# A hybrid decoder block on one core: the first feed-forward block by seven products, its second resident tile later, the residual's bias by DMA, the output sums behind an evacuation

## The chip, the core and the metric

The kernel runs on one core of a Trainium2 chip. The metric is the device time of one execution in microseconds (us); the time of a kernel is the median of its runs. The engines are named as in the profile: PE (TensorE matmul) and PEld (its weight loads), DVE (VectorE), ACT (ScalarE), POOL (GpSimd) and SP (SyncE); POOL and SP issue nearly all the DMAs here.

## The reference, cut to what matters

```python
proj = x @ w_in                      # x: 256 x 2048; w_in: 2048 x 9216
q, k, v, u, vb, ga, gb = split(proj)
attn = dilated_window_attention(q, k, v)           # 8 heads of 128
gmlp = gelu(u) * spatial(layer_norm(gelu(vb)))
merged = sigmoid(ga) * (attn @ w_proj_a) + sigmoid(gb) * (gmlp @ w_proj_b)
h = layer_norm(ALPHA * x + merged @ w_out)         # gain ln1_g, bias ln1_b
a = square(relu(h @ w_ff1 + b_ff1))                # 2048 -> 8192
y = layer_norm(ALPHA * h + a @ w_ff2 + b_ff2)      # 8192 -> 2048
```

All in float32 at a sequence of 256; 99% of the work is in the products with the weights, which are each read once.

## The kernel before, in words

**Products and splits.** A float32 product is made of three products of shorter floats: weight and activation are each split into a high part and a low part, and high x high, high x low and low x high are added up in PSUM. The weights come in chunks of 512 rows x 512 columns (`raw`, 1 MB, three buffers; SP loads chunk j+3 once chunk j is split, line 162). Half a chunk is a piece. A piece's split is two instructions into a ring buffer (`w`): ACT copies the high part (L188), DVE subtracts for the low part (L157, 128x1024). There are six ring buffers (`RING`), and some groups may use further tags while these lie free (`spare`, `wide`).

**Steps.** The program is a list of steps, each of one piece. Before each step the host loop (line 977) emits in this order: the splits that find a free buffer (`emit_splits`); the waiting high and low parts of activations (`rounds`: `hilo`, L93 on ACT and L94 on DVE); one waiting second half of an evacuation (`later`); then the step's matmuls (`run_step`) with the evacuation behind its group's last step; then what `at(step, ...)` has put down for the step. Every engine works its own stream in that order. So a split stands in the streams about six steps ahead of its use, and an evacuation behind what was emitted before it.

**PSUM.** Six banks named `mm`. A group with the weights stationary (`ws`) uses four, so the next group has two free banks and needs the first one's evacuation for its third: ACT copies half of the bank (L273, L275), DVE adds the other half (`sum`, L277).

**Order by stages.** Input projection, attention, gMLP; then for i in 0 to 3 the groups `w_pa` i and `w_pb` i, whose sigmoid gates make `merged`; the output projection; LayerNorm 1; and the feed-forward part in eight blocks of 1024 hidden units: two `ff1` groups a block (eight steps each, F below) and, one block later, `ff2` (E below).

**Seven products.** Of a 1024-row block of `ff2` (and of half of the output projection) the first two column chunks are eight products of 512 rows by 128 tokens by 512 columns. Where the block is in `SUMMED`, they are made by seven: P1 to P7, each on a sum of weights or of activations or both. The weight sums come from accumulating DMAs on POOL's queue into two resident tiles `b` 0 and `b` 1 (`held`): tile 0 is loaded (L624) and gets a further block added (L633) after each of P1, P5 and P6; tile 1 is loaded and gets one block added at once (`held_load`, L626), and serves P7. The activation sums (`ca`) are made by `sum_of_acts`: four DVE operations on 128x128 (`cb`, L576 to L579) for each of four tiles, and their high and low parts. `ORDER` says how P1 to P7 lie among F and E in a block; each P is two steps of six matmuls.

**What the change touches.** `SUMMED` is `range(1, NB - 1)`: block 0 is made by the plain eight products. Its `ff1` groups 2 and 3 come first, then 16 E steps. Between them stands the second residual: `residual2` on DVE makes `ALPHA * ln1_b + b_ff2` (part 0, L562) and then, for each token tile and column chunk, `y * ALPHA * ln1_g` (L565) and the addition of the former (L566); 4 + 8 + 8 operations of 128x512. Its three vectors are broadcast over the partitions by SP (`load_wide`, L556, 1 MB each), behind chunks of `ff1` group 2. The sums for the output projection are made in `ev_yb` when group 1's second half is worked (line 491).

Of the kernel before, what the change touches and what calls it, by code (L numbers as in the profile page):

```python
# [16 lines left out]
ALU = mybir.AluOpType  # L17
# [4 lines left out]
NT = S // P  # L22
# [4 lines left out]
G = 8  # L27
DB = G * 128
FF = 4 * D
CW = 512  # L30
# [5 lines left out]
NCT = CW // P  # L36
ORDER = ("F F F P1 F P1 F F F P5 F P5 F F F P6 F P6 F P3 P3 F P7 F P7 F "
         "E P2 E P2 E E P4 E P4 E E E").split()
WARM = (256, 256, 256, 128)
EARLY = 3  # L40
NBUCKET = 32
MAXDIST = 2048
ALPHA = 2.0 ** 0.25
# [28 lines left out]
def block_kernel(ctx: ExitStack, tc: tile.TileContext, xT, x, w_in, rel_bias, lnv_g, lnv_b, wsT, b_sp,  # L72
# [61 lines left out]
    def add_group(g, sizes=None):  # L134
        hs = add_pieces(g, sizes)
        for h in hs:
            add_step(h, "all", h == hs[0], h == hs[-1])
# [343 lines left out]
    def ev_yb(g):  # L481
        def fin(ot, s):
            if g == 0 and ot == 0:
                tiles["merged"] = quads("merged", [f"S1{i}" for i in range(4)])
            gt, d = tiles["G", g], tiles["merged"][g][:, ot, :]
            nc.vector.tensor_tensor(s, s, gt[:, 1, ot, :], op=ALU.mult)
            q = kept(ot) if g == 0 else s
            nc.vector.tensor_tensor(q, s, gt[:, 0, ot, :], op=ALU.add)
            rounds.append((hilo, d[:, :S], d[:, S:], q))
            if g == 1:  # L490
                sum_of_acts(("S6", "W"), ot, q)

        def ev(ot, p):
            later.append((fin, ot, halves(p)))
        return ev
# [58 lines left out]
    def load_wide(key, src, tag):  # L554
        tiles[key] = big.tile([P, D], F32, name="wide", tag=tag)
        nc.sync.dma_start(tiles[key], bcast(src, D))  # L556

    def residual2(c, part):
        sl = slice(c * CW, (c + 1) * CW)
        bb = tiles["b_ff2"][:, sl]  # L560
        if part == 0:
            nc.vector.scalar_tensor_tensor(bb, tiles["ln1_b"][:, sl], ALPHA, bb, op0=ALU.mult, op1=ALU.add)  # L562
        else:
            y = tiles["y", part - 1][:, sl]
            nc.vector.scalar_tensor_tensor(y, y, ALPHA, tiles["ln1_g"][:, sl], op0=ALU.mult, op1=ALU.mult)  # L565
            nc.vector.tensor_tensor(y, y, bb, op=ALU.add)  # L566

    def sum_of_acts(tags, ot, q):


        if ot == 0:
            for i in range(2):
                tiles["ca", i] = big.tile([P, 2, NCT, 2, P], F32R, name="ca", tag=tags[i])
        q0, t0, t1 = tiles["q", ot], slice(0, P), slice(P, S)
        cb = work.tile([P, 4, P], F32, name="cb", tag="pt")
        nc.vector.tensor_tensor(cb[:, 0], q0[:, t1], q[:, t1], op=ALU.subtract)  # L576
        nc.vector.tensor_tensor(cb[:, 2], q0[:, t0], q0[:, t1], op=ALU.subtract)
        nc.vector.tensor_tensor(cb[:, 1], cb[:, 0], q0[:, t0], op=ALU.subtract)
        nc.vector.tensor_tensor(cb[:, 3], q[:, t0], cb[:, 1], op=ALU.add)  # L579
        for i in range(2):  # L580
            d = tiles["ca", i][:, :, ot]
            rounds.append((hilo, d[:, :, 0], d[:, :, 1], cb[:, 2 * i:2 * i + 2]))

    def kept(ot):
        q = tiles["q", ot] = work.tile([P, S], F32, name="q0", tag="es"[ot // 2])
        return q
# [19 lines left out]
        return ev  # L606

    NB = FF // 1024
    SUMMED = range(1, NB - 1)

    def ff_unit(blk):
        return SimpleNamespace(w=w_ff2, row=blk * 1024, act=lambda r, k: tiles["a", 2 * blk + r][:, k, :],
                               tags=("S10", "S11"), acc="S12", key="ff", scale=None)

    def out_unit():
        return SimpleNamespace(w=w_out, row=0, act=lambda r, k: tiles["merged"][r][:, k, :],
                               tags=("S5", "A0"), acc="A1", key="out", scale=ALPHA)

    def held_load(u, i):

# [74 lines left out]
    def mixed(b):  # L697

        made = {"F": [ff1_group(2 * b), ff1_group(2 * b + 1)], "E": [ff2(b - 1, c) for c in (2, 3)]}
        prods = products(ff_unit(b - 1), ff_unit(b) if b in SUMMED else None)  # L700
        if b - 1 == SUMMED[0]:
            for i in range(2):
                at(len(steps) - 7, held_load, ff_unit(b - 1), i)
        left = {}

        queue = {"F": [], "E": []}
        for name in ORDER:
            if name in prods:
                if name not in left:
                    hs = prods[name]()  # L710
                    left[name] = [(h, h == hs[0], h == hs[-1]) for h in hs]
                q = left[name]
            else:
                q = queue[name]
                if not q:
                    g = made[name].pop(0)
                    for c in range(g.nk // KC):
                        q.append((g, c, None))
                if q[0][2] is None:
                    g, c, _ = q.pop(0)  # L720
                    hs = add_pieces(g, None, (c,))
                    q[:0] = [(h, c == 0 and h == hs[0], c == g.nk // KC - 1 and h == hs[-1]) for h in hs]
            h, f, l = q.pop(0)
            add_step(h, "all", f, l)
# [71 lines left out]
    def quad(key):  # L796
        return lambda k: tiles[key][k // 4][:, k % 4, :]
# [5 lines left out]
    def at(s, f, *a):  # L803
        side.setdefault(s, []).append((f, a))
# [35 lines left out]
    def add_product(name):  # L840
        hs = prods[name]()
        for h in hs:
            add_step(h, "all", h == hs[0], h == hs[-1])

    at(len(steps) + 8, held_load, uo, 0)
    for i in range(4):
        add_group(Group(w_pa, i * CW, 8, quad("attnT"), "ws", ev_ya(i)))
        if i >= 2:
            add_product(("P1", "P6")[i - 2])
        add_group(Group(w_pb, i * CW, 8, quad("gmlpT"), "ws", ev_yb(i), after=start_residual if i == 3 else None))  # L850
        if i == 2:
            at(len(steps), held_load, uo, 1)
            add_product("P5")
# [34 lines left out]
        return Group(w_ff1, f * CW, 16, quad("hT"), "ws", ev_ff1(f))  # L888

    def ff1(f):  # L890
        add_group(Group(w_ff1, f * CW, 16, quad("hT"), "ws", ev_ff1(f), tags=wide if f == 1 else ()))

    def ff2(blk, c):
        return Group(w_ff2, c * CW, 8, lambda k: tiles["a", 2 * blk + k // NCT][:, k % NCT, :], "as",
                     ev_ff2(blk, c), row=blk * 1024, tags=LATE if blk == NB - 1 else ())

    ff1(1)
    s = len(steps)
    for i in range(4):
        for j in range(3):  # L900
            at(s + 13 + 3 * i + j, residual2, i, j)
    for b in range(1, NB):
        j = len(chunks)
        if b - 1 in SUMMED:
            mixed(b)
            continue
        ff1(2 * b)
        ff1(2 * b + 1)
        if b == 1:
            for i, a in enumerate((("ln1_b", ln1_b, "S11"), ("b_ff2", b_ff2, "S10"), ("ln1_g", ln1_g, "S12"))):  # L910
                load_post[j + 2 * i] = [lambda a=a: load_wide(*a)]
        for c in range(4):
            add_group(ff2(b - 1, c))
    at(len(steps), free.extend, LATE[:4])
# [111 lines left out]
```

## Time and profile before

| | |
|---|---|
| runs | 1327.08 us median of 3 (1326.08 to 1327.82) |
| profiled execution | 1327.01 us, of which the span is 1325.3 |
| PE busy | 1312.3 us (99%), 6832 records |
| DVE, ACT, POOL busy | 938.3 (71%), 691.2 (52%), 51.8 (4%) |
| DMA | 288.83 MB, mean 218 GB/s |

A matmul's record lasts longer than its share of PE, since matmuls are pipelined: from the start of one to the start of the next is the time that counts. The idle time before an instruction is given with what ended it.

### The profile page before, as it was taken

What the parts mean: (1) busy time and instruction counts of PE and PEld (TensorE: products, weight loads), DVE (VectorE), ACT (ScalarE), POOL (GpSimd) and SP (SyncE); (2) the same over time, 40 slices, a digit from 0 to 9 for tenths busy, and PEclk for the clock granted to TensorE, in tenths of its full rate; (3) what the DMA queues carried; (4) which work ended last, traced back from release to release, by engine and by line L of the source; (5) the groups of instructions that cost most, each with busy time, mean ns of one, the idle gap of its engine ahead of it and who ended that gap; (6) DMA issues with size and microseconds to landing.
All of it is one profiled execution on the core that took longest, in us unless ns stands there. A gap on an engine that the chain in (4) does not pass through costs nothing. (4 is left out here: it accounts for less than half of the span.)

```text
span 1325.3 us, 17425 instructions
## 1 busy us (share of the span) xinstructions
PE 1312.3 (99%) x6832; PEld 1110.7 (84%) x6832; DVE 938.3 (71%) x1426; ACT 691.2 (52%) x938; POOL 51.8 (4%) x57
## 2 busy tenths in 40 slices
PE   8999999999999999999999999999999999999998
PEld 6888888888888888889888888888888888888886
DVE  6554678565545688888769768678677796786776
ACT  4444465454545565545545356455555565555641
POOL 0000000000000001000000100010000000000000
PEclk9999999999999999999999999999999999999999
DMA  9866545546555559762874988988887879978561
GB/s 321 287 196 206 177 137 181 191 160 222 191 191 190 189 147 274 281 224 68 288 250 156 279 221 286 248 242 252 216 278 234 233 241 255 253 223 236 180 254 64
DMA packets 140003, 288.83 MB, mean 218 GB/s; under 512 B 5256, under 2 KB 7824, under 8 KB 139024
## 3 DMA queue, kind: packets, MB, share of 16 engines
q1 hardware_dynamic: 120592, 240.26, 53.4%
q0 software_dynamic: 19184, 47.20, 16.8%
q8 instruction: 53, 0.87, 0.3%
q14 instruction: 30, 0.25, 0.1%
q10 hardware_dynamic: 144, 0.26, 0.1%
HBM read 285.59 MB, written 2.11 MB: 217 GB/s over the span
## 5 line engine op out<-in xcount | busy, mean ns | idle before, releaser
L157 DVE TENSOR_TENSOR w<-raw,w 128x1024 fp32r<-128x1024 f32 (+1 forms) x438 | 528.5, 1217 | 301.0 <-ACT w L188 300.2
L188 ACT ACTIVATE w<-raw 128x1024 fp32r<-128x1024 f32 (+1 forms) x438 | 456.9, 1053 | 411.5 <-PE mm L254 286.7
L252 PE MATMUL mm<-hT,w 128*128 128x512 f32 x960 | 339.2, 394 | 0.8 <-DVE sum L277 0.8
L252 PE MATMUL mm<-xs,w 128*128 128x512 f32 x896 | 315.7, 395 | 0.0
L254 PE MATMUL mm<-hT,w 128*128 128x256 f32 x1024 | 276.0, 279 | 0.0
L254 PE MATMUL mm<-xs,w 128*128 128x256 f32 x896 | 250.0, 279 | 0.0
L252 PEld LDWEIGHTS mm<-hT,w 128*128 128x128 f32 x960 | 180.0, 187 | 44.2 <-DVE sum L277 1.1
L252 PEld LDWEIGHTS mm<-xs,w 128*128 128x128 f32 x896 | 167.9, 187 | 39.7
L254 PEld LDWEIGHTS mm<-hT,w 128*128 128x128 f32 x1024 | 188.0, 188 | 2.7
L254 PEld LDWEIGHTS mm<-xs,w 128*128 128x128 f32 x896 | 168.0, 187 | 0.2
L242 PE MATMUL mm<-w,a 128*128 128x512 f32 (+1 forms) x328 | 128.1, 390 | 0.0
L241 PE MATMUL mm<-w,a 128*128 128x512 f32 (+1 forms) x328 | 128.0, 390 | 0.0
L240 PE MATMUL mm<-w,a 128*128 128x512 f32 (+1 forms) x328 | 127.8, 390 | 0.0
L157 DVE TENSOR_TENSOR w<-held,w 128x1024 fp32r<-128x1024 f32 x70 | 85.5, 1221 | 40.8 <-ACT w L188 40.4
L188 ACT ACTIVATE w<-held 128x1024 fp32r<-128x1024 f32 x70 | 73.9, 1058 | 64.4 <-PE mm L242 23.7
L240 PEld LDWEIGHTS mm<-w,a 128*128 128x128 f32 x328 | 61.8, 188 | 14.3
L242 PEld LDWEIGHTS mm<-w,a 128*128 128x128 f32 x328 | 61.7, 188 | 14.0
L241 PEld LDWEIGHTS mm<-w,a 128*128 128x128 f32 x328 | 61.8, 188 | 13.9
L240 PE MATMUL mm<-w,xs 128*128 128x512 f32 x120 | 49.5, 412 | 0.4 <-ACT w L188 0.4
L241 PE MATMUL mm<-w,xs 128*128 128x512 f32 x120 | 47.7, 397 | 1.3 <-DVE w L157 1.3
L277 DVE TENSOR_TENSOR sum<-mm,half 128x256 f32<-128x256 f32 x136 | 48.8, 415 | 0.0
L242 PE MATMUL mm<-w,xs 128*128 128x512 f32 x120 | 47.6, 397 | 0.0
(190 smaller groups left out, 1512.3 us busy)
## 6 DMA issues: line engine op xcount, KB each, us to landing
raw<-in_w_ff_dram SPq DMA_DIRECT2D x116, 1024.0 KB, 6.6
raw<-in_w_in_dram SPq DMA_DIRECT2D x68, 1024.0 KB, 5.1
held<-in_w_ff_dram POOLq DMA_DIRECT2D x36, 1024.0 KB, 8.5
raw<-in_w_out_dram SPq DMA_DIRECT2D x14, 1024.0 KB, 5.4
raw<-in_w_pa_dram SPq DMA_DIRECT2D x8, 1024.0 KB, 5.1
raw<-in_w_pb_dram SPq DMA_DIRECT2D x8, 1024.0 KB, 5.1
held<-in_w_out_dram POOLq DMA_DIRECT2D x6, 1024.0 KB, 9.3
raw<-in_w_in_dram SPq DMA_DIRECT2D x6, 512.0 KB, 7.4
```

Source lines behind the costliest of these rows:

```text
L157: nc.vector.tensor_tensor(h["lo"], sl, f32(h["hi"]), op=ALU.subtract)
L188: nc.scalar.activation(h["hi"], source(h), AF.Copy)
L240: nc.tensor.matmul(p, ah, hi[:, kk, cs], start=first and kk == 0, stop=False)
L241: nc.tensor.matmul(p, ah, lo[:, kk, cs], start=False, stop=False)
L242: nc.tensor.matmul(p, al, hi[:, kk, cs], start=False, stop=last and kk == n - 1)
L252: nc.tensor.matmul(p, hi[:, kk, ws_], av, start=st, stop=False)
L254: nc.tensor.matmul(p[:, :S], lo[:, kk, ws_], av[:, :S], start=False, stop=en)
L277: nc.vector.tensor_tensor(s, p[:, :S], t, op=ALU.add)
```

## The change

Block 0 joins `SUMMED`. Its seven products lie by an order of their own, `FIRST`: P3 and P2 ahead of P7, and P7 behind three E steps. Tile 0 is loaded from the step after group 1 of `ff1` begins, tile 1 thirteen steps after that group's end. The three vectors of the residual are loaded ahead of group 1's end, two of them into other buffers (`A2`, `A3`; `b_ff2` into `S11`, which is tile 1's), and group 1 of `ff1` has two further ring buffers in place of four. The residual's 4 + 8 multiplications stand from two steps ahead of the end of group 1 to seven behind it; its 8 additions on DVE go, and two accumulating DMAs of 1 MB on POOL's queue (`residual2_add`, `y` += the 128x2048 tile) come for them. The output projection's sums are no longer made in `ev_yb` but by `at` at four steps from the last of P1 on; `q` is kept in the gate's tile for them.

```diff
+FIRST = ("F F F P1 F P1 F F F P5 F P5 F F F P6 F P6 F P3 P3 F "
+         "E P2 E P2 E F P7 E P7 F E P4 E P4 E E").split()
...
             nc.vector.tensor_tensor(s, s, gt[:, 1, ot, :], op=ALU.mult)
-            q = kept(ot) if g == 0 else s
+
+            q = kept(ot) if g == 0 else gt[:, 0, ot, :] if g == 1 else s
             nc.vector.tensor_tensor(q, s, gt[:, 0, ot, :], op=ALU.add)
             rounds.append((hilo, d[:, :S], d[:, S:], q))
-            if g == 1:
-                sum_of_acts(("S6", "W"), ot, q)
...
             nc.vector.scalar_tensor_tensor(y, y, ALPHA, tiles["ln1_g"][:, sl], op0=ALU.mult, op1=ALU.mult)
-            nc.vector.tensor_tensor(y, y, bb, op=ALU.add)
+
+    def residual2_add(t):
+        nc.gpsimd.dma_start(tiles["y", t], tiles["b_ff2"], accum_op=ALU.add)
...
-    SUMMED = range(1, NB - 1)
+    SUMMED = range(0, NB - 1)
...
-                               tags=("S5", "A0"), acc="A1", key="out", scale=ALPHA)
+                               tags=("S5", "A1"), acc="A0", key="out", scale=ALPHA)
...
-        if b - 1 == SUMMED[0]:
-            for i in range(2):
-                at(len(steps) - 7, held_load, ff_unit(b - 1), i)
...
-        for name in ORDER:
+        for name in FIRST if b == 1 else ORDER:
...
             add_product(("P1", "P6")[i - 2])
+        if i == 2:
+            for k in range(4):
+                at(len(steps) - 1 + k, lambda k=k: sum_of_acts(("S6", "W"), k, tiles["G", 1][:, 0, k, :]))
...
-        add_group(Group(w_ff1, f * CW, 16, quad("hT"), "ws", ev_ff1(f), tags=wide if f == 1 else ()))
+        add_group(Group(w_ff1, f * CW, 16, quad("hT"), "ws", ev_ff1(f), tags=wide[2:] if f == 1 else ()))
...
+    s = len(steps)
+    for i, a in enumerate((("ln1_b", ln1_b, "A2"), ("b_ff2", b_ff2, "S11"), ("ln1_g", ln1_g, "A3"))):
+        at(s + 1 + i, load_wide, *a)
+    at(s + 1, held_load, ff_unit(0), 0)
     ff1(1)
-    s = len(steps)
+    e = len(steps)
     for i in range(4):
-        for j in range(3):
-            at(s + 13 + 3 * i + j, residual2, i, j)
+        at(e - 2 + i // 2, residual2, i, 0)
+        for j in (1, 2):
+            at(e + i + 4 * (j - 1), residual2, i, j)
+    for t in range(NT):
+        at(e + 8, residual2_add, t)
+    at(e + 13, held_load, ff_unit(0), 1)
...
-        if b == 1:
-            for i, a in enumerate((("ln1_b", ln1_b, "S11"), ("b_ff2", b_ff2, "S10"), ("ln1_g", ln1_g, "S12"))):
-                load_post[j + 2 * i] = [lambda a=a: load_wide(*a)]
```

How the streams move, at the three places that the prediction speaks of.

DVE, where the group `w_pa` 2 ends (its four evacuations are `sum<-mm,half x4`, the output sums `cb`); before, the last two of four rounds:

```order
L486 TENSOR_TENSOR sum<-sum,gate 128x256
L488 TENSOR_TENSOR sum<-sum,gate 128x256
L576 TENSOR_TENSOR cb<-q_3906,sum 128x128
L577 TENSOR_TENSOR cb<-q_3906 128x128
L578 TENSOR_TENSOR cb<-cb,q_3906 128x128
L579 TENSOR_TENSOR cb<-sum,cb 128x128
L277 TENSOR_TENSOR sum<-mm,half 128x256 x4
L157 TENSOR_TENSOR w_4193<-raw,w_4193 128x1024
```

and now:

```order
L488 TENSOR_TENSOR sum<-sum,gate 128x256
L491 TENSOR_TENSOR gate<-sum,gate 128x256
L279 TENSOR_TENSOR sum<-mm,half 128x256 x4
L159 TENSOR_TENSOR w_4159<-raw,w_4159 128x1024
L96 TENSOR_TENSOR merged_3822<-gate,merged_3822 128x256
L477 TENSOR_TENSOR gate<-gate,sum 128x256
L159 TENSOR_TENSOR w_4174<-held,w_4174 128x1024
L477 TENSOR_TENSOR gate<-gate,sum 128x256
L579 TENSOR_TENSOR cb<-q_3826,gate 128x128
L580 TENSOR_TENSOR cb<-q_3826 128x128
L581 TENSOR_TENSOR cb<-cb,q_3826 128x128
L582 TENSOR_TENSOR cb<-gate,cb 128x128
```

All four rounds of `cb` now stand behind the evacuation, among the splits for P5 and the next groups.

DVE, from the end of `ff1` group 1 (`sum<-mm,half x4` is its evacuation, `w_5692<-held` and `w_5729<-held` are P1's splits) now:

```order
L159 TENSOR_TENSOR w_5669<-raw,w_5669 128x1024
L563 SCALAR_TENSOR_TENSOR wide<-wide 128x512 x2
L159 TENSOR_TENSOR w_5692<-held,w_5692 128x1024
L279 TENSOR_TENSOR sum<-mm,half 128x256 x4
L563 SCALAR_TENSOR_TENSOR wide<-wide 128x512 x2
L159 TENSOR_TENSOR w_5729<-held,w_5729 128x1024
L601 SCALAR_TENSOR_TENSOR sq<-sum 128x256
L579 TENSOR_TENSOR cb<-q_5470,sq 128x128
L580 TENSOR_TENSOR cb<-q_5470 128x128
L581 TENSOR_TENSOR cb<-cb,q_5470 128x128
L582 TENSOR_TENSOR cb<-sq,cb 128x128
L566 SCALAR_TENSOR_TENSOR y<-y,wide 128x512
```

The residual's first operations, which need two of the loaded vectors, stand ahead of the evacuation of group 1; three more rounds like the last seven rows follow, and behind them this, up to the evacuation of `ff1` group 2:

```order
L566 SCALAR_TENSOR_TENSOR y<-y,wide 128x512
L159 TENSOR_TENSOR w_5884<-held,w_5884 128x1024
L566 SCALAR_TENSOR_TENSOR y<-y,wide 128x512
L159 TENSOR_TENSOR w_5896<-held,w_5896 128x1024
L566 SCALAR_TENSOR_TENSOR y<-y,wide 128x512
L159 TENSOR_TENSOR w_5917<-raw,w_5917 128x1024
L566 SCALAR_TENSOR_TENSOR y<-y,wide 128x512
L159 TENSOR_TENSOR w_5937<-raw,w_5937 128x1024
L159 TENSOR_TENSOR w_5960<-raw,w_5960 128x1024
L159 TENSOR_TENSOR w_5970<-raw,w_5970 128x1024
L279 TENSOR_TENSOR sum<-mm,half 128x256 x4
```

The splits for P5 (`w_5884`, `w_5896`) and for `ff1` group 3 share DVE with the last four multiplications of the residual.

POOL's queue, now, from tile 0 of the first block to tile 1 of the same block (L627 a tile's load, L636 and L629 an accumulation into tile 0 and into tile 1, L569 the residual):

```order
L627 DMA held<-in_w_ff_dram 128x4x512
L636 DMA held<-in_w_ff_dram 128x4x512 x2
L569 DMA y<-wide 128x2048 x2
L636 DMA held<-in_w_ff_dram 128x4x512
L627 DMA held<-in_w_ff_dram 128x4x512
L629 DMA held<-in_w_ff_dram 128x4x512
```

Tile 1's load and accumulation stand behind both additions of the residual, out of whose source buffer the tile is made.

## Rows read from the trace of the kernel before

**Rows 1.** The page: busy us, share of the span and records of each engine.

```profile
PE 1312.3 (99%) x6832; PEld 1110.7 (84%) x6832; DVE 938.3 (71%) x1426; ACT 691.2 (52%) x938; POOL 51.8 (4%) x57
```

**Rows 2.** Waits of PE: who waited for whom, us in total, times, longest.

```profile
PE mm L252 <- DVE sum L277: 2.5, 2, 1.7
...
PE aux L213 <- DVE w L157: 0.3, 1, 0.3
```

**Rows 3.** Timeline of PE at 485: start, us, engine, line, operation, shapes, count [idle].

```profile
485.04 0.40 PE L212 MATMUL aux<-w,merged 128*128 128x512 f32 x1
...
487.84 0.39 PE L252 MATMUL mm<-gmlpT,w 128*128 128x512 f32 x1
...
491.12 0.51 PE L252 MATMUL mm<-gmlpT,w 128*128 128x512 f32 x1 [1.71 <-DVE sum L277]
```

**Rows 4.** Timeline of DVE over the same stretch.

```profile
477.73 0.29 DVE L576 TENSOR_TENSOR cb<-q,sum 128x128 f32<-128x128 f32 x1
...
478.67 1.22 DVE L157 TENSOR_TENSOR w<-raw,w 128x1024 fp32r<-128x1024 f32 x1
...
480.14 0.75 DVE L94 TENSOR_TENSOR ca<-cb,ca 128x256 fp32r<-128x256 f32 x2
480.81 0.42 DVE L486 TENSOR_TENSOR sum<-sum,gate 128x256 f32<-128x256 f32 x1
...
490.65 1.41 DVE L277 TENSOR_TENSOR sum<-mm,half 128x256 f32<-128x256 f32 x4
```

**Rows 5.** Timeline of PE where `ff1` group 1 begins.

```profile
634.21 0.40 PE L252 MATMUL mm<-hT,w 128*128 128x512 f32 x1
...
634.56 0.40 PE L252 MATMUL mm<-hT,w 128*128 128x512 f32 x1
...
636.61 0.50 PE L252 MATMUL mm<-hT,w 128*128 128x512 f32 x1 [0.82 <-DVE sum L277]
```

**Rows 6.** Timeline of DVE at the same place.

```profile
633.86 2.36 DVE L157 TENSOR_TENSOR w<-raw,w 128x1024 fp32r<-128x1024 f32 x2 [1.93 <-ACT w L188]
```

**Rows 7.** Timeline of ACT ahead of P5 of the second block.

```profile
768.18 1.06 ACT L188 ACTIVATE w<-held 128x1024 fp32r<-128x1024 f32 x1 [9.69 <-DMA held<-in_w_ff_dram]
```

**Rows 8.** Timeline of DVE, one round of the residual and `sum_of_acts`.

```profile
705.93 0.42 DVE L598 SCALAR_TENSOR_TENSOR sq<-sum 128x256 f32<-128x256 f32 x1
...
707.33 0.68 DVE L562 SCALAR_TENSOR_TENSOR wide<-wide 128x512 f32<-128x512 f32 x1
707.93 1.22 DVE L157 TENSOR_TENSOR w<-raw,w 128x1024 fp32r<-128x1024 f32 x1
...
710.07 0.41 DVE L598 SCALAR_TENSOR_TENSOR sq<-sum 128x256 f32<-128x256 f32 x1
```

**Rows 9.** One line in a window, a chunk's load: ns of issue, first and last start; landing.

```profile
L145 SPq DMA_DIRECT2D raw<-in_w_ff_dram x1: 368/368/368, 647.8 to 647.8; - x1
...
DMA to landing us min/median/max: 6.6/6.6/6.6
```

**Rows 10.** The same view of the vector's load issued right behind it.

```profile
L556 SPq DMA_DIRECT2D wide<-in_ln_b_dram x1: 497/497/497, 648.2 to 648.2; - x1
...
DMA to landing us min/median/max: 8.8/8.8/8.8
```

**Rows 11.** The same view of L633, accumulation into tile 0, all 21.

```profile
DMA to landing us min/median/max: 8.4/8.6/17.9
```

**Rows 12.** The same view of L626, accumulation into tile 1, the second block's.

```profile
L626 POOL DMA_DIRECT2D held<-in_w_ff_dram x1: 1317/1317/1317, 748.2 to 748.2; - x1
...
DMA to landing us min/median/max: 12.1/12.1/12.1
```

**Rows 13.** The same view of L633, the accumulation issued next.

```profile
L633 POOL DMA_DIRECT2D held<-in_w_ff_dram x1: 1298/1298/1298, 750.2 to 750.2; - x1
...
DMA to landing us min/median/max: 17.9/17.9/17.9
```

**Rows 14.** The same view of L626, all 7.

```profile
DMA to landing us min/median/max: 9.3/10.7/15.2
```

More of the change, by code (lines that the diff above doesn't have):

```diff
@@ L895, in ff2 @@
                      ev_ff2(blk, c), row=blk * 1024, tags=LATE if blk == NB - 1 else ())
+    s = len(steps)
+    for i, a in enumerate((("ln1_b", ln1_b, "A2"), ("b_ff2", b_ff2, "S11"), ("ln1_g", ln1_g, "A3"))):
+        at(s + 1 + i, load_wide, *a)
+    at(s + 1, held_load, ff_unit(0), 0)
     ff1(1)
-    s = len(steps)
+    e = len(steps)
     for i in range(4):
-        for j in range(3):
-            at(s + 13 + 3 * i + j, residual2, i, j)
+        at(e - 2 + i // 2, residual2, i, 0)
[4 more added lines that the diff above has]
+    at(e + 13, held_load, ff_unit(0), 1)
     for b in range(1, NB):
-        j = len(chunks)
         if b - 1 in SUMMED:
```

## The prediction

> **What bounds the kernel now.** I read the page first: PE is busy for 99% of the span [rows 1]. So an edit counts in two ways only, by matmuls that PE no longer makes and by idle time of PE that goes or comes; DVE, busy for 71%, is to be watched where its work comes close to PE's pace. The list of PE's waits gives the idle time inside the run: 2.5 us in two waits for DVE's evacuations, 0.3 in one for a split [rows 2]. The timelines around each show the causes.
>
> At 489.4 PE stands still for 1.71 us [rows 3]: the group `w_pb` 2 wants its third bank, which is free when DVE has added up `w_pa` 2's first bank. DVE comes to that at 490.65 only, behind four rounds of output sums [rows 4].
>
> At 635.8 it stands for 0.82 [rows 5]: `ff1` group 1 wants its third bank, and DVE makes two splits from 633.86 on before it evacuates group 0 [rows 6].
>
> The 0.3 is P5 of the second block, at 770: ACT has waited 9.69 us for tile 0 [rows 7], while the first loads of both tiles were on the queue.
>
> **The change part by part.** Times are on the clock of the trace of before; each stretch is reckoned as if PE had lost nothing ahead of it but what is said.
>
> *Seven products.* Block 0's first two column chunks are 2 groups x 8 k x 2 token tiles x 3 = 96 matmuls of 512 columns before, and 7 products x 4 k x 3 = 84 after. The twelve of one product take PE from 485.04 to 487.84 [rows 3], 0.233 each: minus 2.80.
>
> *Output sums.* One round of `cb` takes 478.67 - 477.73 = 0.94, its low parts 480.81 - 480.14 = 0.67; a split and the low part of `merged` behind it take 1.47, which I divide into 1.13 and 0.34 by their lengths [rows 4]. Without the rounds ahead of it DVE reaches the evacuation at about 485.9, once `w_pa` 2 has ended; the bank is wanted at 489.2. So the 1.71 go. What is late next is P5, which reads the sums: PE comes to it at 499.1. On DVE, from 487.65, where the next split's high part lets it go on, stand 6 splits (6.8), five operations of 0.34 (1.7), four rounds (3.8) and their low parts (2.7): 15.0, so the last low part that P5 wants is written at 502.3. PE wants it at 501.6, in P5's fourth k. I put a wait of 0.7 there (0 to 1.2): minus 1.71, plus 0.7.
>
> *Evacuation of group 0.* Two ring buffers fewer take two splits out of the stream ahead of this evacuation. DVE then makes it at about 632, before PE wants the bank: minus 0.82. The two splits follow by 638 and are wanted at 639.8 and later: nothing.
>
> *Second block's tiles.* Their first loads no longer fall together, since the tiles pass on from block 0: minus 0.33.
>
> *Residual and sums on DVE.* The eight additions that go stand in a stretch in which PE waits for nothing: nothing. But the 12 multiplications move from the E steps to where DVE now makes block 0's sums too, and where P steps want a split every 1.4 us. First the vectors. The chunk ahead of them is issued at about 645.0, when group 1's last split is made, and lands some 5.5 later; a vector behind it lands 657.0 - 654.4 = 2.6 after it [rows 9, 10], so the second vector is there at 655.7. DVE is at the first multiplication at 653 and waits; then come that and a second (0.6 each), P1's split and the evacuation of group 1, begun at 658.05. PE began group 1 at 634.21, a step is eight pairs of 0.35 [rows 5], and so it wants the third bank of group 2 at 634.2 + 22.5 + 1.4 = 658.1 and gets it at 658.5.
>
> From there DVE does not rest: evacuation 1.3, two multiplications 1.2, a split 1.1, until 661.7; four rounds of 4.14, each a square, `cb`, a multiplication, a split and the low parts [rows 8], until 678.3; then four multiplications (2.4) and six splits (6.8), until 687.5. The first bank of group 2 is free at 688.0. PE wants it 8 F steps (22.5), four halves of P (5.6) and two tiles (1.4) after 656.7, at 686.2. So PE has lost 1.8 there in all; with a semaphore's passing I take 1.9. If the vectors are there by 653 it is 0.4, if they come 2 us later than I put it, 3.9. It can't be a gain, since no wait of PE's stands in that stretch before.
>
> *Tile 1.* POOL's queue is a chain: P5's accumulation, two residual additions, P6's accumulation, tile 1's load, tile 1's accumulation, P7. P5's second split ends at 681.8; an accumulation of 1 MB takes 8.6 from its issue [rows 11], about 2 of it before data moves: 690.7. The residual's additions are not in the trace. From below, a vector's load, of their size and their 8 KB rows, follows its forerunner by 2.6 [rows 9, 10]; from above, of two accumulations issued at 748.2 and 750.2 [rows 12, 13] one lands at 760.3, the other at 768.1, 7.9 later, with chunks in between. Alone it would be 8.6 - 2 = 6.6, with 2 KB rows. I take 5, nearer to the accumulation than to the load, and less for the longer rows: 700.7. P6's accumulation (6.6) ends at 707.3, the load 2.6 behind it; tile 1's accumulation, issued at 710.3, takes 10.7 [rows 14], until 721.0. ACT and DVE have split the tile by 723.3. PE wants it, 28 steps (64.5 us) and the lost 1.9 after 656.7, at 723.1 and its low part 0.2 later. So nothing. At 2.6 an addition nothing too, at 6.6 3.2, at 7.9 5.8.
>
> The two accumulations 2 us apart, beside chunks, took 12.1 and 17.9 [rows 12, 13] in place of 8.6 [rows 11]. The Trainium skill, page "DMA: Bandwidth & Descriptors", section "Issuing engines are not separate DMA queues", has it that DMAs run on the same 16 engines and interleave, whichever engine issued them. That agrees with these rows and speaks against an addition by DMA being free: by this rule the chain would run near 7.9 an addition.
>
> *Sum.* -2.80 - 1.71 + 0.7 - 0.82 - 0.33 + 1.9 = -3.1. The profiled execution took 1327.01 us, 1.7 more than its span and 0.07 less than the median of the runs, so the sum from it stands for the median too: **1324.0 us**. Its own range, from the wait at P5 and the vectors' landing, is 1322.4 to 1325.5.
>
> **The rivals.**
>
> *The covers hold in full.* The vectors are there when DVE comes to them, and P5 does not wait: -2.80 - 1.71 - 0.82 - 0.33 + 0.4 = -5.3, 1321.7. For it: SP's queue has one chunk alone ahead of them. Against it: DVE gets there eight us after that chunk's issue, and chunk and two vectors take 5.5 + 2 x 2.6.
>
> *Wait for wait.* The residual's additions cost what an accumulation alone costs, 6.6, and P7 waits 3.2: 1327.2, no change. For it: no accumulation shown is quicker. Against it: theirs are 2 KB rows.
>
> *P7 waits long.* One mechanism, the chain of accumulations under load: 7.9 for each addition, and for tile 1's own accumulation the 15.2 that is the largest of its row [rows 14]. That is 5.8 + 4.5 on the sum: 1334.3, slower. It decides from the point where the chain comes 5.7 later than I put it. For it: the 17.9 above. Against it: of 28 accumulations few are so late.
>
> **How the numbers follow.** Forecast 0.50, covers in full 0.20, wait for wait 0.22, long wait 0.08. A difference of 0.2%, 2.65 us, is about what a measurement can tell from none; that line is at 1324.4. Two thirds of the forecast's chance lie below it: faster 0.20 + 0.33 = 0.53; the same 0.17 + 0.22 = 0.39; slower 0.08. The range, 1321.5 to 1328.0, leaves out the long wait and little of the others.
>
> **What would show it.** Right: 12 matmuls of 512 columns fewer at the same pace; no idle PE at the third bank of `w_pb` 2 and of `ff1` group 1; under 1.2 us at P5 of the output projection; DVE idle on a DMA before its first residual multiplication, then full for some 30 us; 1 to 3 us of idle PE between the third banks of groups 2 and 3, put down to DVE; ACT waiting some 9 us for tile 1, and PE hardly at all. Wrong: PE idle by more than 2 us at P7 (the additions are dearer than 5 us each); DVE not idle before the residual (the vectors land early); or a pause at a place not named here, such as P6, whose tile lands 4 us ahead of need by this count.

## The result and the profile after

The changed kernel took 1334.76 us in the median of 4 runs (1333.94 to 1335.5), the kernel before 1327.15 beside it: 1.0058 times as long, 95% interval 1.0045 to 1.0071. Forecast were 1324.0, so it is 10.8 us slower than forecast. The profiled execution took 1334.82, 1333.1 of it the span; before, 1327.01 [rows 1].

The page of the changed kernel: busy us, share of the span and records of each engine.

```profile
PE 1314.1 (99%) x6820; PEld 1110.1 (83%) x6820; DVE 947.2 (71%) x1451; ACT 699.7 (52%) x952; POOL 60.5 (5%) x65
```

The twelve matmuls are gone (6820 for 6832), and yet PE is busy for longer: some matmuls have become slower. The waits of PE between 480 and 800 us, in us in total, times, longest:

```profile
PE aux L214 <- ACT w L190: 3.9, 1, 3.9
PE mm L254 <- DVE sum L279: 1.9, 2, 1.1
PE mm L242 <- ACT w L190: 1.0, 1, 1.0
PE aux L215 <- DVE w L159: 0.9, 2, 0.8
PE mm L243 <- DVE w L159: 0.8, 1, 0.8
PE aux L216 <- DVE ca L96: 0.5, 1, 0.5
```

The old waits [rows 2] are gone. In their place stand two that were forecast (L216, P5's; L254, DVE's lag) and four that were not: two pairs of ACT and DVE splits that come late. The timeline of PE at these places (start, us, engine, line, operation, shapes, count, idle time before it and what ended it):

```profile
501.43 0.39 PE L215 MATMUL aux<-w,ca 128*128 128x512 f32 x1
502.34 0.50 PE L216 MATMUL aux<-w,ca 128*128 128x512 f32 x1 [0.52 <-DVE ca L96]
...
656.73 0.28 PE L256 MATMUL mm<-hT,w 128*128 128x256 f32 x1
658.12 0.50 PE L254 MATMUL mm<-hT,w 128*128 128x512 f32 x1 [1.11 <-DVE sum L279]
...
686.52 0.28 PE L256 MATMUL mm<-hT,w 128*128 128x256 f32 x1
687.59 0.50 PE L254 MATMUL mm<-hT,w 128*128 128x512 f32 x1 [0.79 <-DVE sum L279]
...
702.99 0.28 PE L256 MATMUL mm<-hT,w 128*128 128x256 f32 x1
707.12 0.49 PE L214 MATMUL aux<-w,ca 128*128 128x512 f32 x1 [3.86 <-ACT w L190]
708.38 0.80 PE L215 MATMUL aux<-w,ca 128*128 128x512 f32 x1 [0.77 <-DVE w L159]
...
709.40 0.63 PE L214 MATMUL aux<-w,ca 128*128 128x512 f32 x1
709.83 0.63 PE L215 MATMUL aux<-w,ca 128*128 128x512 f32 x1
...
711.42 0.40 PE L216 MATMUL aux<-w,ca 128*128 128x512 f32 x1
...
715.04 0.28 PE L256 MATMUL mm<-hT,w 128*128 128x256 f32 x1
716.31 0.49 PE L242 MATMUL mm<-w,a 128*128 128x512 f32 x1 [0.99 <-ACT w L190]
717.57 0.50 PE L243 MATMUL mm<-w,a 128*128 128x512 f32 x1 [0.77 <-DVE w L159]
...
721.56 0.39 PE L244 MATMUL mm<-w,a 128*128 128x512 f32 x1
```

Read from start to start. At 702.99 P3 wants its chunk's high part: 4.13 pass in place of 0.12, then 1.26 in place of 0.23 until the low part is there. After that the matmuls follow each other by 0.43 in place of 0.23, at 1.2 instead of 2.4 GHz: eight of them from 708.38 to 711.42 take 3.04 in place of 1.87. At 715.04 an E step meets the same: 1.27 in place of 0.12, 1.26 in place of 0.23, and ten matmuls to 721.56 in 3.99 in place of 2.33. Together 4.01 + 1.03 + 1.17 + 1.15 + 1.03 + 1.66 = 10.05 us lost, of which 2.8 are the clock. That is nearly all of the 10.8 that separate the result from the forecast.

Why the splits are late, the timeline of ACT says:

```profile
706.01 1.06 ACT L190 ACTIVATE w<-raw 128x1024 fp32r<-128x1024 f32 x1 [8.94 <-DMA raw<-in_w_ff_dram]
...
715.20 1.06 ACT L190 ACTIVATE w<-raw 128x1024 fp32r<-128x1024 f32 x1 [6.88 <-DMA raw<-in_w_ff_dram]
```

ACT was idle for 8.94 and 6.88 us until a chunk of weights landed. The three chunks that SP issued from 685.0 to 697.8 (the line with its count, ns of issue, first and last start; then the time from issue to landing):

```profile
L147 SPq DMA_DIRECT2D raw<-in_w_ff_dram x3: 367/367/367, 685.0 to 697.8; - x3
...
DMA to landing us min/median/max: 19.9/21.0/27.9
```

In the kernel before, the four chunks issued in nearly the same stretch took a quarter of that:

```profile
L145 SPq DMA_DIRECT2D raw<-in_w_ff_dram x4: 367/368/368, 688.2 to 706.0; - x4
...
DMA to landing us min/median/max: 5.1/5.1/5.2
```

What lay beside them now are the two additions of the residual on POOL's queue:

```profile
L569 POOL DMA_DIRECT2D y<-wide x2: 852/1162/1472, 682.6 to 684.4; - x2
...
DMA to landing us min/median/max: 13.4/15.5/17.6
```

The first landed at 682.6 + 13.4 = 696.0, the second at 684.4 + 17.6 = 702.0; the first of the three chunks came only after both, at 706.0. The windows of this stretch (busy us of each engine, then the granted clock of PE, the DMA engines' busy share and GB/s):

```profile
690.00:702.00 12.00, 12.00 (x66) 10.26 (x65) 6.98 (x11) 5.64 (x8) 1.29 (x1) 1.00 1.02 230
702.00:708.00 6.00, 1.76 (x9) 1.04 (x7) 0.90 (x1) 1.99 (x3) 0.79 (x1) 0.99 1.10 260
708.00:716.00 8.00, 6.94 (x27) 5.49 (x27) 1.80 (x3) 1.12 (x2) 0.65 (x1) 0.80 1.04 378
716.00:724.00 8.00, 6.92 (x22) 5.31 (x23) 7.50 (x7) 5.71 (x7) 0.62 (x1) 0.79 1.09 275
```

and the first of them before:

```profile
690.00:702.00 12.00, 12.00 (x70) 10.44 (x70) 8.55 (x11) 5.39 (x8) 0.00 (x0) 1.00 0.59 191
```

Before, the 16 engines were busy for 0.59 of the time; now they are full (1.02 and more; records of packets overlap, so a share can pass 1) from 690 to 724, and from 690 to 702, at 230 GB/s, they carry little more than the 191 of before. The chunks are what comes short.

### The profile page after: what moved, and what is told of

Same layout as the page of the kernel before. It is cut to its first block, busy times and chain, and to the rows that moved or that the text cites. A ratio compares the mean times of both kernels' runs of the same rounds, so it can differ in the third digit from the quotient of the medians.

```text
span 1333.1 us, 17464 instructions
## 1 busy us (share of the span) xinstructions
PE 1314.1 (99%) x6820; PEld 1110.1 (83%) x6820; DVE 947.2 (71%) x1451; ACT 699.7 (52%) x952; POOL 60.5 (5%) x65
## 4 chain that ended last, share of the span: by engine, by line
PE 91%; DVE 4%; DMA 4%; ACT 1%; issue 0%; SPq 0%; DVEq 0%; ACTq 0%
PE mm L254 34%; PE mm L256 18%; PE mm L243 9%; PE mm L244 9%; PE mm L242 9%; PE aux L216 4%; PE aux L214 4%; PE aux L215 3%; DMA raw<-in_w_ff_dram 2%; DVE w L159 2%; PE mm L259 1%; DMA wide<-in_b_ff_dram 1%; DMA raw<-in_w_in_dram 1%; DMA xraw<-in_xT_dram 0%; DVE ca L96 0%
## 5 line engine op out<-in xcount | busy, mean ns | idle before, releaser
L254 PE MATMUL mm<-hT,w 128*128 128x512 f32 x960 | 340.0, 394 | 1.9 <-DVE sum L279 1.9
L254 PE MATMUL mm<-xs,w 128*128 128x512 f32 x896 | 315.7, 395 | 0.0
L254 PEld LDWEIGHTS mm<-hT,w 128*128 128x128 f32 x960 | 180.0, 187 | 45.7 <-DVE sum L279 2.5
L254 PEld LDWEIGHTS mm<-xs,w 128*128 128x128 f32 x896 | 167.9, 187 | 39.9
L159 DVE TENSOR_TENSOR w<-held,w 128x1024 fp32r<-128x1024 f32 x80 | 97.8, 1222 | 36.9 <-ACT w L190 36.6
L242 PE MATMUL mm<-w,a 128*128 128x512 f32 (+1 forms) x296 | 115.9, 392 | 1.0 <-ACT w L190 1.0
L243 PE MATMUL mm<-w,a 128*128 128x512 f32 (+1 forms) x296 | 116.0, 392 | 0.8 <-DVE w L159 0.8
L190 ACT ACTIVATE w<-held 128x1024 fp32r<-128x1024 f32 x80 | 83.9, 1057 | 62.6 <-PE mm L244 22.9
L244 PE MATMUL mm<-w,a 128*128 128x512 f32 (+1 forms) x296 | 115.9, 392 | 0.0
L242 PEld LDWEIGHTS mm<-w,a 128*128 128x128 f32 x296 | 56.0, 189 | 14.2 <-ACT w L190 1.3
L243 PEld LDWEIGHTS mm<-w,a 128*128 128x128 f32 x296 | 56.2, 190 | 13.6 <-DVE w L159 1.1
L244 PEld LDWEIGHTS mm<-w,a 128*128 128x128 f32 x296 | 56.1, 190 | 12.7
L214 PE MATMUL aux<-w,ca 128*128 128x512 f32 x128 | 51.1, 399 | 3.9 <-ACT w L190 3.9
L215 PE MATMUL aux<-w,ca 128*128 128x512 f32 x128 | 51.4, 402 | 0.9 <-DVE w L159 0.9
L216 PE MATMUL aux<-w,ca 128*128 128x512 f32 x128 | 51.1, 399 | 0.5 <-DVE ca L96 0.5
L242 PE MATMUL mm<-w,xs 128*128 128x512 f32 x120 | 49.5, 412 | 0.5 <-ACT w L190 0.5
```

What stands on the lines that cost most here:

```text
L159: nc.vector.tensor_tensor(h["lo"], sl, f32(h["hi"]), op=ALU.subtract)
L190: nc.scalar.activation(h["hi"], source(h), AF.Copy)
L214: nc.tensor.matmul(p, ah, hi[:, kk], start=first and kk == 0, stop=False)
L215: nc.tensor.matmul(p, ah, lo[:, kk], start=False, stop=False)
L216: nc.tensor.matmul(p, al, hi[:, kk], start=False, stop=last and kk == n - 1)
L242: nc.tensor.matmul(p, ah, hi[:, kk, cs], start=first and kk == 0, stop=False)
```

## The experiments

Theory A: the residual's two accumulating DMAs take the engines' time from the chunk loads, and PE's 10 us follow from that. Rivals: the new order of block 0 asks for chunks faster than they come (B); DVE's backlog splits them late, so that their buffers come free late (C). Ratios are to the kernel before, which took 1327.2 to 1327.4 beside them, with 95% intervals.

**1. Without the additions.**

```diff
-    for t in range(NT):
-        at(e + 8, residual2_add, t)
```

> The changed kernel without the two residual additions by DMA (the output lacks ln2's input bias, alpha times ln1's plus ff2's). Theory A, the two additions on POOL's queue starve the chunk loads of SP's queue: chunks issued at 685 and 687 land in under 10 us instead of 21.0 and 27.9, PE's waits of 3.86 and 0.77 (at 703) and 0.99 and 0.77 (at 715) go, and with them the stretches at half clock: 9 to 10 us less than 1334.8, so 1324.5 to 1326.5. Rival B, the new order of block 0 asks for chunks faster than the queue brings them, whatever lies beside it: waits stay, 1331 or more. Rival C, DVE's backlog of residual multiplications splits the chunks late, so that their buffers come free late: waits stay, 1333 or more.

1324.83 us, ratio 0.9985 (0.9975 to 0.9995). 9.9 us are the additions', and with them out the time stands 0.8 from the forecast. P3 and the E step wait no more, PE keeps its full clock; two low parts by DVE, at P2 and P7, still come late, by 1.2 in all. B and C are out as the cause of these 10 us. The same chunks:

```profile
L147 SPq DMA_DIRECT2D raw<-in_w_ff_dram x3: 367/368/368, 683.9 to 697.6; - x3
...
DMA to landing us min/median/max: 8.3/8.7/11.7
```

They still take longer than the 5.1 of before, and that belongs to the rest of the change. Nor is it a full share by itself that costs: without the additions the engines are as full from 702 to 724 (1.03 to 1.08), and PE hardly waits. They carry more in that time, from 702 to 708 for instance 392 GB/s where it was 260:

```profile
702.00:708.00 6.00, 6.00 (x32) 5.06 (x31) 1.32 (x2) 0.07 (x1) 0.00 (x0) 1.00 1.03 392
```

**2. The additions on DVE.**

```diff
+    def residual2_add(t, c):
+        y = tiles["y", t][:, c * CW:(c + 1) * CW]
+        nc.vector.tensor_tensor(y, y, tiles["b_ff2"][:, c * CW:(c + 1) * CW], op=ALU.add)
...
+    for i in range(8):
+        at(e + 9 + i // 2, residual2_add, i // 4, i % 4)
```

> The residual's bias added by DVE again, in eight additions of 512 columns, two a step in the four steps behind P5's first half (where the two DMAs stood). Theory A: chunks land in under 10 us and no half clock, as without any addition; DVE gets 8 x 0.6 = 4.8 us more work in a stretch in which it rests about 3 us of 10, so PE may lose up to 2: 1325.5 to 1328. Rival B (order): 1331 or more. Rival C (DVE's backlog): longer than the changed kernel, 1336 or more.

1326.23, ratio 0.9992 (0.9983 to 1.0002): 8.5 less than by DMA. As expected by A; the chunks land after 7.5 to 10.9.

**3. The same bytes in eight DMAs of 2 KB rows.**

```diff
-        nc.gpsimd.dma_start(tiles["y", t], tiles["b_ff2"], accum_op=ALU.add)
+        for c in range(4):
+            sl = slice(c * CW, (c + 1) * CW)
+            nc.gpsimd.dma_start(tiles["y", t][:, sl], tiles["b_ff2"][:, sl], accum_op=ALU.add)
```

> The same bytes added by DMA at the same place, but as eight DMAs of 128x512 (2 KB rows) in place of two of 128x2048 (8 KB rows). Theory A in its packet form (the two queues take turns packet by packet, so a chunk's 2 KB goes once for every 8 KB of the addition): the chunks land in 10 to 15 us, the wait at P3 falls below 1 us and PE stays at full clock; POOL's chain gets longer, P7 may wait up to 3: 1326 to 1330. Theory A in its byte form (what starves the chunks is the time the 16 engines need for 2 MB of accumulation, however cut): waits as before or longer, 1334 to 1340.

1337.60, ratio 1.0080 (1.0065 to 1.0095): the byte form's number, but the trace shows a bit of both. The first two chunks do land sooner, after 14.3 and 19.6 where it was 21.0 and 27.9:

```profile
L147 SPq DMA_DIRECT2D raw<-in_w_ff_dram x3: 367/368/368, 685.4 to 698.6; - x3
...
DMA to landing us min/median/max: 14.3/16.7/19.6
```

and P3 does not wait. But the last addition, issued at 691.7, lands 16.8 later, at 708.5 in place of 702.0, and what is queued behind pays: P2 (its first matmul reads `a`) and P7 (`ca`) wait, as the timeline of PE says.

```profile
716.49 0.80 PE L214 MATMUL aux<-w,a 128*128 128x512 f32 x1 [3.91 <-ACT w L190]
...
734.48 0.51 PE L214 MATMUL aux<-w,ca 128*128 128x512 f32 x1 [3.15 <-ACT w L190]
```

The clock falls there too, to 0.57 from 716 to 724. Shorter rows share the engines more evenly and use more of their time (the packet records in the next section show both); the delay moves on, and grows.

**4. Plain copies instead of accumulations**, `accum_op` left out.

> The two DMAs of 1 MB at the same place, of the same 8 KB rows, but plain copies in place of accumulations (y is overwritten by the bias, so the output is another). Theory A, packet form: a plain packet of 8 KB takes about half as long as an accumulating one, so the starving is about half: P3 waits 0 to 2 us, 1326 to 1330. If only accumulation does harm (a read, an addition and a write on the engine): no wait, 1324.5 to 1326. If it is only that SP's queue is second to POOL's, however long the packets: 1332 to 1335.

1327.56, ratio 1.0006 (0.9997 to 1.0015), 2.7 above no DMA at all and 7.2 below the accumulations. The three chunks land after 13.2 to 14.6, P3 does not wait, P2 for 1.20 and 0.77, and the clock falls behind that (0.83 from 716 to 724). The packet form gave this time; it is the middle case: accumulation is what makes it dear, but not that alone.

**5. Half the dose**: the first 128 tokens by DMA, the others by DVE.

```diff
+    at(e + 8, residual2_add, 0)
+    for i in range(4):
+        at(e + 9 + i // 2, residual2_add, 1, i)
```

> Half the dose: the addition for the first 128 tokens by DMA as in the changed kernel, the one for the other 128 by DVE (four operations in two steps behind it). If the cost is in proportion to the engine time of the accumulations: half of the 8.5 us between the changed kernel and the one with all additions on DVE, so 1330 to 1331.5. If a chunk's buffer covers the first few us and only what goes beyond it costs (each addition moves the chunks by 5.7 to 5.9, and PE waited 3.86 at P3): hardly any wait at P3 and no half clock, 1326 to 1328.

1327.33, ratio 1.0001 (0.9991 to 1.0010): 1.1 above all on DVE, 7.4 below all by DMA. The cost is not in proportion: the three raw buffers cover the first addition, the second goes beyond them. The waits of PE between 640 and 760 hold none for a chunk:

```profile
PE mm L254 <- DVE sum L279: 1.9, 1, 1.9
PE aux L215 <- DVE w L159: 0.8, 1, 0.8
```

with chunks that land after this long:

```profile
DMA to landing us min/median/max: 13.2/13.7/13.9
```

The first two of these took 8.3 and 7.5 with all additions on DVE, so one addition held them back by 4.9 and 6.4. The 1.1 that is left need not come from them: behind the wait of 1.9, pairs of matmuls follow each other by 0.64 in place of 0.35 from 688.8 to 692.0, some 1.5 us by the clock (0.82 from 690 to 696).

**6. The output sums alone**, put on the kernel before (`ev_yb`, the four `at`, and the two buffers exchanged, as in the change's diff).

> The kernel before with one part of the change alone: the output sums made behind the evacuations of w_pb 2 (and, since these now read the gate in A1 later, tile 1 in A1 and the sums of products in A0). By the prediction's terms, with the wait at P5 as the changed kernel's trace shows it: minus 1.71, plus 0.5 to 0.8, so about 1 us less than before, 1326.0 to 1326.6. If the terms of the first stage are what went wrong: 1327 or more.

1326.26, ratio 0.9993 (0.9983 to 1.0003), 1.1 below the 1327.36 beside it. In its trace the 1.71 [rows 3] is gone and 0.5 at P5 has come, as forecast for this term; the time alone, with an interval that reaches past 1, would not show it.

**7. Early vectors.** The three vectors are loaded when `ff1` group 0 begins, the twelve multiplications stand in group 1, the additions on DVE as in experiment 2.

```diff
+    for a in (("ln1_b", ln1_b, "S12"), ("b_ff2", b_ff2, "S11"), ("ln1_g", ln1_g, "S13")):
+        at(len(steps) + 3, load_wide, *a)
...
-        add_group(Group(w_ff1, f * CW, 16, quad("hT"), "ws", ev_ff1(f), tags=wide[2:] if f == 1 else ()))
+        add_group(Group(w_ff1, f * CW, 16, quad("hT"), "ws", ev_ff1(f), tags=spare[2:4] if f == 1 else ()))
...
+        at(e - 7 + i // 2, residual2, i, 0)
...
+            at(e - 5 + (i + 4 * (j - 1)) // 2, residual2, i, j)
```

> Additions on DVE (two a step in the four steps behind P5's first half), and in addition the three vectors loaded at the start of ff1 group 0 (12 to 25 us earlier, into S12, S11 and S13; group 1's splits get A2 and A3 instead) and all twelve residual multiplications made in ff1 group 1. If DVE's late start on the vectors is the cause of the wait at the third bank of group 3 (2.0 us with the additions on DVE): it goes, and the waits at P3 (0.27 and 0.77) and P7 (0.30) stay: 1324.0 to 1324.6. If the sums of block 0 are too much for DVE by themselves: 1325.5 to 1327.

1324.06, ratio 0.9970 (0.9959 to 0.9981), and once more, beside other kernels:

> The kernel with early vectors and all additions on DVE once more, beside the two others: 1323.5 to 1324.5, 0.25% less than before.

1322.90, ratio 0.9971 (0.9960 to 0.9983), 0.6 below the range that was expected. This version beats both kernels: 0.3% below before. The 2.0 at the third bank of group 3 is gone, but so are the waits at P3 and P7 that were expected to stay; the first number fits its range in part by chance. What is left between 480 and 800 us is this (the first of the two runs):

```profile
PE mm L254 <- DVE sum L279: 0.6, 1, 0.6
PE aux L216 <- DVE ca L96: 0.5, 1, 0.5
```

**8. Early vectors, and tile 1 nine steps earlier**, with the additions on DVE at e - 1 to e + 2.

```diff
+    for i in range(8):
+        at(e - 1 + i // 2, residual2_add, i // 4, i % 4)
+    at(e + 4, held_load, ff_unit(0), 1)
```

> As the one with early vectors, but with the additions on DVE in the four steps around the start of block 0 (e - 1 to e + 2), so that tile 1 is free and loads nine steps earlier, at about 668 instead of 698, where the 16 engines are busy for half the time. If what is left of the waits at P3 and P7 (about 1.3 us) comes from tile 1's 2 MB beside P6's accumulation and the chunks: it goes, 1322.5 to 1323.5. If the additions make DVE late once more: 1324 to 1326.

1331.30, ratio 1.0027 (1.0017 to 1.0036): a miss, 8 above the range hoped for and 5 above the other. It is the engines' load once more, but the loser is another: P5's accumulation, which P6 needs, now stands behind tile 1's on POOL's own queue (issued 679.9, landed 689.1) and shares the engines with chunks. P5's accumulation (L637) by its issue and landing:

```profile
L637 POOL DMA_DIRECT2D held<-in_w_ff_dram x1: 1272/1272/1272, 681.4 to 681.4; - x1
...
DMA to landing us min/median/max: 15.8/15.8/15.8
```

ACT, which splits the tile, in its timeline:

```profile
697.17 1.06 ACT L190 ACTIVATE w<-held 128x1024 fp32r<-128x1024 f32 x1 [10.67 <-DMA held<-in_w_ff_dram]
```

and the timeline of PE at P6's first matmul:

```profile
698.28 0.79 PE L214 MATMUL aux<-w,ca 128*128 128x512 f32 x1 [4.27 <-ACT w L190]
```

The clock falls behind this wait (0.74 from 700 to 710).

**9. Early vectors, and the additions by DMA eight steps earlier** (`at(e, residual2_add, t)`), tile 1 where the change has it.

> Early vectors and multiplications, and the additions by DMA after all, with the same two accumulations of 8 KB rows, but eight steps earlier (step e instead of e + 8): behind P1's accumulation, at about 662 to 682, where the 16 engines are busy for 0.5 to 0.86 of the time. Theory A (what starves the chunks is engine time that falls into a stretch where the engines are full already): P3 waits about 1 us at most, no half clock, 1322.5 to 1325. If an accumulation between two tiles on chip starves SP's queue wherever it stands: chunks of 20 us again, 1330 or more.

1327.16, ratio 0.9998 (0.9989 to 1.0008): neither number. The chunks beside the additions are slow here too:

```profile
L147 SPq DMA_DIRECT2D raw<-in_w_ff_dram x3: 367/367/368, 666.1 to 678.7; - x3
...
DMA to landing us min/median/max: 14.9/16.7/16.9
```

but they are wanted later. PE waits 0.8 and 0.8 at P2, with the clock at 0.83 from 710 to 720 behind it, and 1.4 at the third bank of group 3, which DVE evacuates late because its splits wait 5.5 for a chunk. So the place decides the price, though not whether chunks are slowed; against experiment 7 the DMAs still cost 3 to 4 us.

**10. As 7, with two of the multiplications behind the evacuation of group 1.**

> Early vectors, additions on DVE, and the last two of the twelve multiplications made one step later, behind the evacuation of ff1 group 1 instead of ahead of it. The wait of 0.57 at the third bank of group 2 goes, since DVE comes to that evacuation 1.28 us earlier; the 1.28 us come back behind it, where DVE has no wait of PE's within reach: 0.4 to 0.7 less than the kernel with all twelve ahead. If DVE's backlog then ends late at group 3's third bank: as that kernel or 1 us more.

1324.28, ratio 0.9975 (0.9966 to 0.9985): no gain. The wait at the third bank of group 2 is 1.2 here and 1.0 beside it in the kernel of experiment 7, and DVE comes to that evacuation hardly earlier, at 657.06 against 657.38. It is late from before: at 639.4 ACT has waited 2.06 us for a chunk, and only 0.67 in the kernel beside it. So in the profiled execution the 1.28 us taken off DVE's list went into a chunk that came later; whether it did so in the other runs is not known, and what the two multiplications are worth there stays open.

## Why the prediction was wrong, step by step

**The step that failed** is "Tile 1" with its sentence "So nothing". It weighed the residual's additions only as links of POOL's chain ahead of P7. But the same 2 MB run on the engines that carry SP's chunks, and there they cost 9.9 us. The rows for it were on the table: [rows 12, 13] show accumulations of 12.1 and 17.9 "with chunks in between" in place of 8.6. I read these as chunks that slow the accumulations, and never asked what the accumulations do to the chunks. The Trainium skill, page "DMA: Bandwidth & Descriptors", section "Issuing engines are not separate DMA queues", says that DMAs of all issuers share the 16 engines and interleave; the prediction quoted it against the chain's price alone. The traces agree with it in both directions: with the additions as the only difference (experiment 1), chunks of 8.3 to 11.7 became chunks of 19.9 to 27.9.

The chain itself was priced too low as well, and that P7 did not wait is luck. The additions landed 6.0 apart, where 5 was taken; tile 1's load (issued 702.5, 12.4 long) landed 5.0 behind P6's accumulation, where 2.6 was taken; and tile 1's accumulation, by its issue and landing,

```profile
L629 POOL DMA_DIRECT2D held<-in_w_ff_dram x1: 1272/1272/1272, 715.3 to 715.3; - x1
...
DMA to landing us min/median/max: 11.3/11.3/11.3
```

was there at 726.6 in place of 721.0. That is 5.6 late, just short of the 5.7 from which the prediction let its rival of a long wait decide. It cost nothing because PE, which had lost its 10 us by then, came to P7 at 733.24 in place of 723.1:

```profile
733.24 0.40 PE L214 MATMUL aux<-w,ca 128*128 128x512 f32 x1
```

Even without the additions (experiment 1) the tile landed at 721.3, so the other links were too cheap by about what the additions were reckoned at.

The rival "P7 waits long" came out at 1334.3, close to the measured time, by another mechanism: it had PE waiting at P7 for tile 1. PE did not wait there, and that the two times are near each other is chance.

**The other steps**, from the trace of the changed kernel:

| step | forecast | measured |
|---|---|---|
| twelve matmuls | -2.80 | 12 fewer |
| third bank of `w_pb` 2 | -1.71 | gone |
| P5 of the output projection | +0.7 | +0.68 (501.43 to 502.34, less 0.23) |
| evacuation of group 0 | -0.82 | gone |
| P5 of the second block | -0.33 | gone |
| DVE's lag | +1.9 | +2.2 (656.73: 1.27, 686.52: 0.95) |
| tile 1 for P7 | nothing | nothing, with the tile 5.6 late and PE 10.1 late |
| chunks of P3 and of the E step behind it | not seen | +7.2, and +2.8 by the clock |

The two profiled executions differ by 7.8; with 2.80 for the twelve matmuls and the waits that are gone at their size, the right column adds up to 7.2.

Two sums of the prediction do not come out. For P5 of the output projection, 487.65 + 15.0 is 502.65 and not 502.3, so the terms stood for a wait of 1.05. DVE did write the last low parts until 502.63, but PE went on at 502.34, behind the first of them; that 0.7 was hit so closely is luck. And by the ends that are given for this wait and for the vectors, the sum's own range is 1321.8 to 1326.5 and not 1322.4 to 1325.5. Neither bears on the step that failed.

Of DVE's lag the sum is right and the division is not: 0.4 was forecast at the third bank of group 2 and it was 1.27. The changed kernel is 1.0 ahead here (1.71 - 0.68); with that put back, the second vector was there at 656.3 (forecast 655.7) and DVE at the evacuation at 658.65 (forecast 658.05), so the vector's 0.6 is most of the difference. The timeline of DVE:

```profile
655.30 1.29 DVE L563 SCALAR_TENSOR_TENSOR wide<-wide 128x512 f32<-128x512 f32 x2 [2.87 <-DMA wide<-in_b_ff_dram]
656.51 1.22 DVE L159 TENSOR_TENSOR w<-held,w 128x1024 fp32r<-128x1024 f32 x1
657.65 1.45 DVE L279 TENSOR_TENSOR sum<-mm,half 128x256 f32<-128x256 f32 x4
```

The last paragraph of the prediction named the sign: "a pause at a place not named here". Nothing in it would have led there: each edit was checked against the engine or the queue that it sits on, and what the 16 engines have to carry in a stretch, busy for 0.59 of it before and given two additions, three chunks and a tile, was not worked out.

**How the engines divided their time** can be counted from the packet records of the traces, one record for a row. While both queues had work, the engines took about as many records from one as from the other, whatever their length:

| stretch | POOL's queue: records, us each | SP's queue: records of 2 KB, us each |
|---|---|---|
| changed kernel, 691 to 701 | 217 (8 KB, added), 0.64 | 244, 0.10 |
| experiment 4, 691 to 696 | 202 (8 KB, copied), 0.32 | 216, 0.08 |
| experiment 3, 691 to 708 | 1049 (2 KB, added), 0.177 | 1136, 0.097 |

An addition of 1 MB is 128 rows of 8 KB; with one record of a chunk for each, the 16 engines need 128 x (0.64 + 0.10) / 16 = 5.9 us for it, and it landed 6.0 behind the one before. Only a quarter of a chunk's 512 rows passes meanwhile. Copies need 3.2 in the same way, and landed 3.3 apart. In rows of 2 KB, the two additions need 17.5, took 17.4 (691.1, when P5's accumulation had landed, to 708.5), and let two whole chunks pass. So both forms of theory A in experiment 3 hold a part: the turns decide what the chunks get, and four short records (0.71) cost more than a long one (0.64). The Trainium skill, page "DMA: Bandwidth & Descriptors", section "Queues, rings and completion order", has each engine take turns between queues packet by packet. The counts agree with it; whether a turn is one record or several they do not tell.

**What stays open.** Turns are not the whole delay: from 685 to 689, right behind its issue, the first chunk got no record at all beside the 400 of P5's accumulation, and in experiment 1 it was the same from 684 to 687. Why, no run shows.

## What to carry to other kernels

Work that is moved from a compute engine to a DMA does not become free: add up what the DMA engines have to carry in the 20 us after its issue, and ask first what it does to the loads that were there, then what they do to it. Here an accumulating DMA of 1 MB between two on-chip tiles held back chunk loads by 4.9 and 6.4 us; one of them disappeared under three buffers, two did not. And a wait of PE costs more than itself where the clock falls behind it: here 2.8 on top of 7.2.

## What the runs showed of the hardware that was not expected

- Beside chunk loads, an addition of 1 MB by an accumulating DMA between two tiles on chip landed 6.0 us behind the one before it (696.0 to 702.0); a record of 8 KB took 0.64 us when added and 0.32 when copied, and plain copies of the same rows gave back 7.2 of 9.9 us.
- Rows of 2 KB in place of 8 KB made the two additions land at 708.5 instead of 702.0, with the engines' share at 1.10 in place of 1.02 between 690 and 702.
- PE fell to 1.2 GHz after waits of 3.86 and 0.77, and again after 0.99 and 0.77 some nine us later; after a single 0.76 at P2, at 711.8, in experiment 1 the granted clock of 708 to 716 stayed at 1.00. After one wait of nearly 2 us at the third bank of group 3 it fell in experiment 5 (0.82 from 690 to 696) and did not in experiment 2 (1.00), so the length of a wait alone does not tell it.
